# Starting a normed part of a transformer kernel: which engine splits the weights, into which buffers, and in what order

## The chip, the cores and the metric

The kernel runs on one core of a Trainium2 chip. The metric is the device time of one launch in microseconds (us); lower is better. It is written in Tile, which places the semaphores and the buffers; the order of the instructions is the compiler's, but for the stretches that the code marks as ordered by hand.

## What is computed

256 tokens of 1024 features go through eight parts, one after the other, all in float32: a SwiGLU feed-forward, a hybrid mixer, two feed-forwards, a sparse attention, a feed-forward, and two three-branch mixers. Each part normalises its input, multiplies it with a wide weight matrix, and adds its result to the residual `x`:

```python
def rms_norm(x, g):
    y = x * lax.rsqrt(jnp.mean(x * x, axis=-1, keepdims=True) + EPS) * g
for l in range(DEPTH):
    x = x + 0.5 * swiglu(rms_norm(x, ffn_norm[l, 0]), ...)
    h = rms_norm(x, mix_norm[l])
    x = x + (hybrid_mixer(h, ...) if l % 2 == 0 else sparse_attention(h, ...))
    x = x + 0.5 * swiglu(rms_norm(x, ffn_norm[l, 1]), ...)
```

The two three-branch mixers follow, with norms of the same form.

## The kernel before

**Products.** A float32 operand is held as the sum of two float32r parts, hi and lo, and a product is three matmuls (`mm3`, L273 to L278: hi hi, hi lo, lo hi). Weights come from memory in tiles `raw` of [128, 2048]; each is used as two halves of 1024 columns. `Net.halve` (L259) takes a pair of buffers, one of tag `hi` and one of tag `lo` (four of each), and `split` (L199) fills them: ScalarE (ACT) copies the 1024 columns into hi, and two subtractions of 512 columns make lo. The second of these goes to GpSimd (POOL) where `help` is set, and to VectorE (DVE) else.

**The start of a part.** `down_steps` (L333) is the last product of a part. It holds its last four weight halves a, b, c, d, and finishes one token tile at a time: `whole(t, a)`, `whole(t, b)` are six matmuls each, `last(t, cb)` is six more and then `done`, one DVE addition that writes 512 columns of `x` of token tile t. Between these products the next part is begun (class `Entry`, L47 to L101), in an order written out by hand (L370 to L407): `manual()` makes PE, DVE, ACT and POOL each keep the order in which the code names their work. A part either has its input normed first (`norm` is true: the hybrid, the sparse attention and the two last mixers, so four starts) or takes the norm later (the feed-forwards).

The steps of a normed start, for token tile t:

- `square(t, cb)` (L68): ACT squares 512 columns of `x` and sums them.
- `root(t)` (L79): two small POOL instructions (L212, L215) make 1/sqrt of the mean.
- `scale(t)` (L82): two DVE instructions (L85) of 512 columns multiply `x` by the root and the gain.
- `turn(t, b)` (L95): PE transposes four blocks of 128 columns (L433), ACT copies them out as the hi of the input (L201), DVE makes the lo (L205).
- `halve(i)` (L92): the split of half i of the part's first weights; i = 0, 1 come from the first `raw` tile, 2 and 3 from the second.
- `go(kk, t)` (L99): three matmuls with k-tile kk of token tile t and weight half kk // 2.

Before, in the four normed starts, `HELP[1]` is all ones, so that the second lo of each of the four halves is POOL's. The halves take their buffers from the tags `hi` and `lo`: these are held by a, b, c and d, so half 0 waits for the end of `whole(1, a)`, half 1 for that of `whole(1, b)`, and halves 2 and 3 for that of `last(1, 1)`.

**Other storage.** Wide work tiles come from tag `g` with 13 buffers of [128, 1024]. In a normed start after a feed-forward, the feed-forward's last hidden activations hold four of them and the start takes seven (gain 1, transposed input 4, scaled input 2).

Of the kernel before, what the change touches and what calls it, by code (L numbers as in the profile page):

```python
# [10 lines left out]
F32R = mybir.dt.float32r  # L11
# [4 lines left out]
PSUM = bass.MemoryType.PSUM  # L16

D = 1024
# [6 lines left out]
HELP = ((0, 0, 0, 0), (1, 1, 1, 1), (1, 1, 0, 0))  # L25
# [3 lines left out]
class Wide:  # L29
    """Transposed activations, split in two float32r parts: k-tiles of [128 features, 256 tokens]."""  # L30
# [16 lines left out]
class Entry:  # L47
    """The start of a part: its input, normed or not, transposed (times the gain), and its first
    512 columns. gain [128, 8], or all of it on every partition where the norm is taken here."""

    def __init__(self, net, i, norm, dram, between=None):
        self.net, self.nc, self.norm, self.first = net, net.nc, norm, not i
        self.raw, self.gain = [], net.gain
        self.load(dram[0], between)
        if not between:
            self.load(dram[1])
        if i:
            self.gain = net.g()
            self.nc.sync.dma_start(self.gain, net.ins["gains"][i])
        self.hT, self.w = Wide(net.g, 2), []  # L60
        self.ss = [net.small(2) for _ in range(2)]
        self.src, self.rstd = [net.g() for _ in range(2)] if i else net.x, [None, None]
        self.out = [net.ps() for _ in range(2)]
# [28 lines left out]
    def halve(self, i):  # L92
        self.w.append(self.net.halve(self.raw[i // 2], i % 2, HELP[2 if self.first else self.norm][i]))

# [8 lines left out]
class Net:  # L103
# [52 lines left out]
    def consts(self):  # L156
# [8 lines left out]
        self.tri = self.const(128)                   # [s, t] = s <= t  # L165
        nc.vector.tensor_scalar(self.tri, ij, 0.0, None, op0=OP.is_ge)
        self.after = self.const(128)                 # [s, t] = s > t
        nc.vector.tensor_scalar(self.after, ij, 0.0, None, op0=OP.is_lt)
        self.cap = self.const(128)                   # 0 where s <= t, else very negative
        nc.scalar.activation(self.cap, self.after, AF.Copy, scale=-BIG)  # L170
        # [t, s]: very large where s <= t, else very negative
# [13 lines left out]
    def narrow(self, dram, cols, hT, out):  # L185
        """A few columns of h @ W, token-major, into out[:, t, :]. dram: [128, 8 * cols]."""
# [20 lines left out]
    def rsqrt(self, v, n, scale=1.0, add=EPS):  # L207
        """1 / sqrt(v * scale + add), [128, n]; add may be a column."""
# [9 lines left out]
    def row_rstd(self, x):  # L218
        """[128, 1] of 1/sqrt(mean(x*x) + eps), x [128, 1024]."""
# [6 lines left out]
    def softplus(self, y, n):  # L226
        """max(y, 0) + log1p(exp(-|y|)); log1p(u) = 2 atanh(u / (2 + u)) as a series (|argument| <= 1/3)."""
# [31 lines left out]
    def halve(self, raw, h, help=False):  # L259
        """Half h of the columns as (hi, lo)."""  # L260
        self.n += 1
        c = raw.shape[-1] // 2
        hi = self.wp.tile([128, 1024], F32R, name=f"hi{self.n}", tag="hi", bufs=4)[:, :c]
        lo = self.wp.tile([128, 1024], F32R, name=f"lo{self.n}", tag="lo", bufs=4)[:, :c]
        self.split(hi, lo, raw[:, h * c:(h + 1) * c], help)
        return hi, lo

    def unit(self, dram, cols=2048, help=(0, 0)):
        """Load [128, cols], give two (hi, lo) halves."""
# [3 lines left out]
    def mm3(self, out, a, b, start, stop):  # L273
        """out += a^T b with a = (hi, lo), b = (hi, lo)."""
# [5 lines left out]
    def group_x(self, dram, hT):  # L280
        """512 columns of h @ W, token-major: one PSUM bank per token tile.
        dram: [2, 128, 2048] (k half; 4 k-tiles x 512 columns)."""
# [7 lines left out]
    def group_steps(self, dram, hT):  # L290
        """group_x in two steps, a yield in between."""
# [14 lines left out]
    def weave(self, main, side, done):  # L306
        """Emit main, with as many steps of side as it gives in between; done gets an item when main is through."""
# [7 lines left out]
    def group_w(self, dram, hT):  # L315
        """256 columns of h @ W, feature-major: two PSUM tiles, [128, :256] used.
        dram: [128, 2048] (8 k-tiles x 256 columns)."""
# [15 lines left out]
    def down_steps(self, dram, n, aT, done, then, ready={}, mid=lambda: None):  # L333
        """x-wide product: aT(kk, t) -> (hi, lo) stationary; dram [n/2, 128, 2048]
        (2 k-tiles x 1024 columns). done(t, cb, psum) when half a token tile is complete;
        the next part (then) starts as the last k-tiles, a token tile at a time, go through.
        mid finishes the second token tile of these."""
# [32 lines left out]
        with self.manual():  # L370
# [3 lines left out]
            if E.norm:  # L374
# [4 lines left out]
                E.root(0)  # L379
                E.scale(0)  # L380
                whole(1, a)
                E.halve(0)
                whole(1, b)
                last(1, 0)
                E.turn(0, 0)
                E.halve(1)
                last(1, 1)
                E.halve(2)
                E.turn(0, 1)
                E.square(1, 0)  # L390
                E.square(1, 1)
# [32 lines left out]
    def to_T(self, t, src, aT, gain=None):  # L424
        """src [128 tokens, 1024] -> k-tiles of aT for token tile t (times gain[:, k])."""
# [3 lines left out]
    def flip(self, src, aT, b, t, gain=None):  # L429
        """src [128 tokens, 512] -> half b of aT, token tile t."""  # L430
# [5 lines left out]
    def put_T(self, p, aT, b, t, gain):  # L436
        """Transposed [128, 4, 128] in PSUM (times gain) -> half b of aT, token tile t."""
# [4 lines left out]
        # the two engines take turns at a PSUM bank: each all of it at a time  # L442
# [37 lines left out]
    def start(self, dram):  # L480
        """The first part's start: loads in the order of their use; the clock of TensorE is up by then."""
# [57 lines left out]
class Hybrid:  # L539
    def hybrid(self, then):  # L540
# [8 lines left out]
        def products():  # L549
            """The wide products that only wait for the input: z, q, k, v and the output gate."""  # L550
# [30 lines left out]
        def chain():  # L581
            """Gives how many steps of the wide products may go in here."""
# [38 lines left out]
            bc = self.g().rearrange("p (j t c) -> p j t c", j=4, t=2)     # B0 B1 C0 C1  # L621
# [10 lines left out]
            def inputs(g):  # L632
                """x of one group of 8 heads, token-major, before its activation"""
# [9 lines left out]
            def states(g):  # L643
# [4 lines left out]
                # state after the first chunk: B^T (x dt decay)  # L648
# [7 lines left out]
            def decays(g):  # L656
                """per chunk of 128 tokens: scores times decays [s, head, t]"""
# [44 lines left out]
            # scores C B^T (transposed), B of the first chunk token-major  # L702
# [32 lines left out]
            R = self.t2()                   # R0 R1 wi wk rows  # L735
# [13 lines left out]
            w = self.small(16)              # exp(-m_t) (2 chunks), w_inter, state weights  # L749
# [25 lines left out]
            # state of the first chunk  # L775
# [55 lines left out]
def _parts(x, n, bits):  # L831
    """x as a sum of n float32 parts of so many significant bits."""
# [18 lines left out]
class Sparse:  # L851
    def rope_setup(self):
        """cos and sin of position * frequency, [128, 2, 32] each."""
# [14 lines left out]
        self.cs = self.const(128)           # cos (2 x 32), sin (2 x 32)  # L868
# [4 lines left out]
        # tables (c, s) times the gain of q; times that of k, and plain for the index key  # L873
# [15 lines left out]
    def rope(self, out, x, c, s, H, copies=1, help=0):  # L889
        """out[:, h, copy, :] = x rotated; c, s [128, H or 1, 2, 32] broadcast; x [128, H, 64]."""  # L890
# [14 lines left out]
    def sparse(self, then):  # L905
# [10 lines left out]
        kv = self.l2().rearrange("p (t c) -> p t c", t=2)  # L916
        wi = self.small(16).rearrange("p (t h) -> p t h", t=2)
        kT = self.l2().rearrange("p (i t s) -> p i t s", i=2, t=2)      # key, index key; twice over the partitions
        v = kv[:, :, 64:128]
        kk = self.t2().rearrange("p (h r d) -> p h r d", h=4, r=2)    # (t, i), twice  # L920
# [45 lines left out]
        def index_logits(t):  # L966
            S = 128 * (t + 1)
            for jb in range(2):
                for r in range(2):              # heads on one half of the partitions share a bank
# [23 lines left out]
        def choose(t, part):  # L993
            """The 64 largest scores of a row: 0 there, very negative elsewhere."""
# [49 lines left out]
        cat = Wide(self.f, 2)  # L1044

        def attend(t, g, b):
            """Some heads: scores with the bias, and their maxima."""
            S = 128 * (t + 1)
            per = 4 // (t + 1)                  # heads in one PSUM bank
            if b == 0:  # L1050
                state[t, g] = (v8(self.pt()), self.small(8), self.small(8), self.small(8))
            po, sm, mx, nm = state[t, g]        # by parity
# [22 lines left out]
        def probs(t, g, b):  # L1075
            """Their transposes."""
# [8 lines left out]
        def values(t, g, b):  # L1085
            """Their products with the values."""
# [51 lines left out]
class Second:  # L1138
    def second_setup(self):
        nc, V, A, G = self.nc, self.nc.vector, self.nc.scalar, self.nc.gpsimd  # L1140
        self.rtri = self.const(128)                  # [s, t] = s >= t
        V.tensor_tensor(self.rtri, self.after, self.ident, OP.add)
        self.before = self.const(128)                # [s, t] = s < t
        V.tensor_tensor(self.before, self.tri, self.ident, OP.subtract)
        self.rcap = self.const(128)                  # 0 where s >= t, else very negative
# [9 lines left out]
        self.near = self.load_const("near", 128)     # in one block of 32  # L1155
        self.eye = self.load_const("eye", 512)       # [q, i] = 2 q + (p / 32) % 2 == i
        rel = self.t2(512, I32)
        G.iota(rel.rearrange("p (j i) -> p j i", j=2), pattern=[[-128, 2], [1, 256]], base=0, channel_multiplier=-1)
        self.rel = self.const(512)                   # [j, i] = i - j
        G.tensor_copy(self.rel, rel)  # L1160
        # log sigmoid of the decays: [128, layer, direction, head]
# [6 lines left out]
    def second(self, l, then, end=None):  # L1168
# [13 lines left out]
        # ================= gated delta rule =================  # L1182
        def delta(y_c):
            """Gives how many steps of the other branches may go in here."""
# [15 lines left out]
            V.reciprocal(beta, eb)                   # [t, direction, head]  # L1200
            gs = self.small(16)                      # log decays: [direction, t, head]
# [583 lines left out]
```

## Time and profile before

| | |
|---|---|
| median of 3 runs | 1735.54 us |
| lowest and highest of them | 1732.81 and 1738.21 us |
| span of the profiled execution | 1757.1 us |
| instructions in it | 23334 |

The page gives no other time for the profiled execution than its span, which is 21.6 us above the median of the runs. In the views below, PE is TensorE, PEld its weight loads, DVE VectorE, ACT ScalarE, POOL GpSimd. A time "from the span's start" is where an instruction stood in this execution. PEclk is the granted clock of TensorE as a share of 2.4 GHz.

### The profile page before, as it was taken

To read this page: it belongs to the slowest core of one execution; us is meant where nothing else is said; L and a number is where in the kernel's file an instruction comes from. 1 tells how busy PE (TensorE), PEld (TensorE's weight loads), DVE (VectorE), ACT (ScalarE), POOL (GpSimd) and SP (SyncE) were. 2 spreads that over 40 slices of the span, in tenths; PEclk is the share of its full clock that TensorE was granted. 3 is DMA by queue.
4 is the path that set the end of the run, shared out by engine and by line. 5 is a ranking of instruction groups with operands and counts; after the bars stand their busy time and mean duration, and the time that the engine had idled before them with its cause. 6 is when DMAs were issued, how large, how long until landed. Compare 5 with 4: busy or idle time off the path is not lost.

```text
span 1757.1 us, 23334 instructions
## 1 busy us (share of the span) xinstructions
PE 1720.3 (98%) x8742; PEld 1437.8 (82%) x8742; DVE 1111.6 (63%) x2107; ACT 902.7 (51%) x1323; POOL 318.1 (18%) x466
## 2 busy tenths in 40 slices
PE   9999999999999999999899999999999999999998
PEld 7888799887888888887688888788898878879886
DVE  6555588666555565547736564557775765678565
ACT  6544476465444454435445544466446446745643
POOL 3000121001000100002311000233632124264211
PEclk9999999999999999999669999999999999999999
DMA  7545453445455554554114555455544444544442
GB/s 269 189 173 199 146 192 121 144 158 185 173 191 191 180 184 176 193 188 151 40 66 174 192 174 216 140 174 168 156 145 150 158 155 168 168 134 167 156 144 96
DMA packets 63425, 287.40 MB, mean 164 GB/s; under 512 B 23760, under 2 KB 26704, under 8 KB 30288
## 3 DMA queue, kind: packets, MB, share of 16 engines
q1 hardware_dynamic: 63312, 285.92, 46.5%
q8 instruction: 68, 1.11, 0.3%
q14 instruction: 45, 0.37, 0.1%
HBM read 283.28 MB, written 2.62 MB: 163 GB/s over the span
## 4 chain that ended last, share of the span: by engine, by line
PE 81%; POOL 6%; DVE 4%; issue 4%; DMA 2%; ACT 2%; SPq 1%; POOLq 0%; ACTq 0%; DVEq 0%
PE mm L277 24%; PE mm L278 24%; PE mm L276 24%; POOL g L1320 2%; POOL g L1318 2%; PE tr L433 1%; PE tr L468 1%; DMA g<-dram 1%; ACT hi L201 1%; DVE lo L205 1%; POOL lo L205 1%; DMA dram<-g 1%; DVE g L85 1%; POOL sm L215 0%; DVE g L987 0%
## 5 line engine op out<-in xcount | busy, mean ns | idle before, releaser
L205 DVE TENSOR_TENSOR lo<-raw,hi 128x512 fp32r<-128x512 f32 (+1 forms) x1024 | 694.8, 720 | 406.1 <-ACT hi L201 404.6
L201 ACT ACTIVATE hi<-raw 128x1024 fp32r<-128x1024 f32 x530 | 551.5, 1045 | 455.3 <-PE mm L278 317.7
L277 PE MATMUL mm<-lo,g 128*128 128x512 f32 (+1 forms) x1440 | 576.9, 401 | 0.8 <-DVE lo L205 0.5
L276 PE MATMUL mm<-hi,g 128*128 128x512 f32 (+1 forms) x1440 | 576.5, 403 | 0.7 <-ACT g L201 0.7
L278 PE MATMUL mm<-hi,g 128*128 128x512 f32 (+1 forms) x1440 | 571.5, 397 | 0.3 <-DVE g L446 0.2
L278 PEld LDWEIGHTS mm<-hi,g 128*128 128x128 f32 x1440 | 273.8, 190 | 62.8 <-DVE g L205 1.6
L277 PEld LDWEIGHTS mm<-lo,g 128*128 128x128 f32 x1440 | 274.0, 190 | 61.5 <-DVE lo L205 3.9
L276 PEld LDWEIGHTS mm<-hi,g 128*128 128x128 f32 x1440 | 273.9, 190 | 60.2 <-ACT g L201 1.2
L277 PE MATMUL mm<-lo,f 128*128 128x512 f32 x416 | 165.2, 397 | 0.2 <-POOL lo L205 0.2
L278 PE MATMUL mm<-hi,f 128*128 128x512 f32 x416 | 164.8, 397 | 0.0
L276 PE MATMUL mm<-hi,f 128*128 128x512 f32 x416 | 163.6, 400 | 0.0
L276 PE MATMUL mm<-g,hi 128*128 128x256 f32 x480 | 136.3, 284 | 0.0
L278 PE MATMUL mm<-g,lo 128*128 128x256 f32 x480 | 135.8, 285 | 0.0
L277 PE MATMUL mm<-g,hi 128*128 128x256 f32 x480 | 135.2, 282 | 0.0
L212 POOL TENSOR_SCALAR sm<-sm 128x1 f32<-128x1 f32 x18 | 9.4, 521 | 562.2 <-ACT c L70 561.1
L277 PEld LDWEIGHTS mm<-lo,f 128*128 128x128 f32 x416 | 78.4, 188 | 19.0 <-POOL lo L205 0.6
L278 PEld LDWEIGHTS mm<-hi,f 128*128 128x128 f32 x416 | 78.3, 188 | 18.5
L276 PEld LDWEIGHTS mm<-hi,f 128*128 128x128 f32 x416 | 78.5, 189 | 18.2
L276 PEld LDWEIGHTS mm<-g,hi 128*128 128x128 f32 x480 | 90.6, 189 | 0.7 <-issue 0.2
L277 PEld LDWEIGHTS mm<-g,hi 128*128 128x128 f32 x480 | 90.5, 189 | 0.3
L278 PEld LDWEIGHTS mm<-g,lo 128*128 128x128 f32 x480 | 90.1, 188 | 0.4 <-issue 0.2
L201 ACT ACTIVATE g<-tr 128x512 fp32r<-128x512 f32 x48 | 28.1, 595 | 86.9 <-PE tr L433 57.1
(387 smaller groups left out, 1693.9 us busy)
## 6 DMA issues: line engine op xcount, KB each, us to landing
raw<-in_wgu_dram SPq DMA_DIRECT2D x86, 1024.0 KB, 4.8
raw<-in_wdn_dram SPq DMA_DIRECT2D x44, 1024.0 KB, 4.8
raw<-in_bx_dram SPq DMA_DIRECT2D x24, 1024.0 KB, 4.9
raw<-in_bgate_dram SPq DMA_DIRECT2D x24, 1024.0 KB, 4.9
raw<-in_bw_dram SPq DMA_DIRECT2D x20, 1024.0 KB, 5.0
raw<-in_hyx_dram SPq DMA_DIRECT2D x12, 1024.0 KB, 4.8
raw<-in_bproj_dram SPq DMA_DIRECT2D x12, 1024.0 KB, 5.0
raw<-in_hyw_dram SPq DMA_DIRECT2D x10, 1024.0 KB, 4.8
```

The lines of the kernel that those rows point to most:

```text
L85: self.nc.vector.scalar_tensor_tensor(self.src[t][:, s], self.net.x[t][:, s], self.rstd[t], self.gain[:, s], op0=OP.mult, op1=OP.mult)
L201: nc.scalar.activation(hi, src, AF.Copy)
L205: (nc.gpsimd if o and help else nc.vector).tensor_tensor(lo[..., s], src[..., s], hi[..., s].bitcast(F32), OP.subtract)
L212: G.tensor_scalar(r, v, add, EPS, op0=OP.add, op1=OP.add)
L276: mm(out, a[0], b[0], start=start, stop=False)
L277: mm(out, a[0], b[1], start=False, stop=False)
L278: mm(out, a[1], b[0], start=False, stop=stop)
L433: self.nc.tensor.transpose(p[:, k, :], src[:, k * 128:(k + 1) * 128], self.ident)
L468: nc.tensor.transpose(p[:, t, j, :], hd[:, j * 128:(j + 1) * 128], self.ident)
L1318: G.tensor_tensor(a, Z[:, :m, e:e + 1].to_broadcast([128, m, n]), B[:, e:e + 1, cs].to_broadcast([128, m, n]), OP.mult)
L1320: G.tensor_tensor(Z[:, :m, cs], Z[:, :m, cs], a, OP.add)
```

## The change

The flag for a normed part no longer selects a row of `HELP`: only the very first part, which is not one of the four, has POOL's help. `Net.halve` can be given a pair of buffers, and half 1 gets two of tag `g`. The hand-written order of a normed start is another. Comments and docstrings are gone too.

```diff
-HELP = ((0, 0, 0, 0), (1, 1, 1, 1), (1, 1, 0, 0))
+HELP = ((0, 0, 0, 0), (1, 1, 0, 0))
...
-    def halve(self, i):
-        self.w.append(self.net.halve(self.raw[i // 2], i % 2, HELP[2 if self.first else self.norm][i]))
+    def halve(self, i, spare=False):
+
+        self.w[i] = self.net.halve(self.raw[i // 2], i % 2, HELP[self.first][i],
+                                   [self.net.g(1024, F32R) for _ in range(2)] if spare else None)
...
-    def halve(self, raw, h, help=False):
+    def halve(self, raw, h, help=False, home=None):
...
-        hi = self.wp.tile([128, 1024], F32R, name=f"hi{self.n}", tag="hi", bufs=4)[:, :c]
-        lo = self.wp.tile([128, 1024], F32R, name=f"lo{self.n}", tag="lo", bufs=4)[:, :c]
+        hi, lo = home or (self.wp.tile([128, 1024], F32R, name=f"{p}{self.n}", tag=p, bufs=4)[:, :c] for p in ("hi", "lo"))
...
                 last(0, 1)
                 E.square(0, 1)
                 E.root(0)
+                E.halve(1, True)
+                whole(1, a)
                 E.scale(0)
-                whole(1, a)
                 E.halve(0)
                 whole(1, b)
+                E.turn(0, 0)
                 last(1, 0)
-                E.turn(0, 0)
-                E.halve(1)
+                E.square(1, 0)
+                E.halve(2)
                 last(1, 1)
-                E.halve(2)
+                E.square(1, 1)
                 E.turn(0, 1)
-                E.square(1, 0)
-                E.square(1, 1)
                 E.root(1)
                 E.halve(3)
                 E.scale(1)
```

After these lines, unchanged: `go(0, 0)` to `go(6, 0)`, `turn(1, 0)`, `go(7, 0)`, `turn(1, 1)`, and the eight `go(kk, 1)`.

## Rows read from the trace of the kernel before

**Rows 1.** The page, parts 1 and 4: busy time by engine; the chain that ended last.

```profile
PE 1720.3 (98%) x8742; PEld 1437.8 (82%) x8742; DVE 1111.6 (63%) x2107; ACT 902.7 (51%) x1323; POOL 318.1 (18%) x466
...
PE 81%; POOL 6%; DVE 4%; issue 4%; DMA 2%; ACT 2%; SPq 1%; POOLq 0%; ACTq 0%; DVEq 0%
```

**Rows 2.** Waits of PE, whole span: total us, times, longest us.

```profile
PE tr L433 <- DVE g L85: 8.1, 8, 1.8
```

**Rows 3.** Windows, the four normed starts: us, PE busy (instructions), PEclk, DMA share, GB/s.

```profile
194.64:210.09 15.45, 13.38 (x66) 1.00 0.26 82
789.89:805.33 15.44, 13.36 (x65) 1.00 0.16 40
1116.96:1133.44 16.48, 14.44 (x65) 0.93 0.30 103
1429.95:1445.28 15.33, 13.37 (x66) 1.00 0.27 86
```

**Rows 4.** Timeline of PE, first normed start: start us, duration us, instruction, idle before it.

```profile
197.42 0.40 PE L276 MATMUL mm<-hi,g 128*128 128x512 f32 x1
...
198.58 0.40 PE L278 MATMUL mm<-hi,g 128*128 128x512 f32 x1
199.28 0.66 PE L433 MATMUL tr<-c,g 128*128 128x128 f32 x4 [0.30 <-DVE g L85]
199.69 0.48 PE L276 MATMUL mm<-hi,g 128*128 128x512 f32 x1
...
201.52 0.48 PE L276 MATMUL mm<-hi,g 128*128 128x512 f32 x1
...
206.38 0.40 PE L278 MATMUL mm<-hi,g 128*128 128x512 f32 x1
208.54 0.66 PE L433 MATMUL tr<-c,g 128*128 128x128 f32 x4 [1.76 <-DVE g L85]
208.95 0.48 PE L276 MATMUL mm<-hi,g 128*128 128x512 f32 x1
...
209.73 0.60 PE L433 MATMUL tr<-c,g 128*128 128x128 f32 x4
210.09 0.48 PE L276 MATMUL mm<-hi,g 128*128 128x512 f32 x1
```

**Rows 5.** Timeline of DVE, just before and in the first normed start.

```profile
187.63 1.29 DVE L205 TENSOR_TENSOR lo<-raw,hi 128x512 fp32r<-128x512 f32 x2 [1.49 <-ACT hi L201]
...
197.46 2.43 DVE L85 SCALAR_TENSOR_TENSOR g<-x,sm,g 128x512 f32<-128x512 f32 x2 [1.92 <-POOL sm L215]
...
202.81 1.19 DVE L205 TENSOR_TENSOR lo<-raw,hi 128x512 fp32r<-128x512 f32 x1
```

**Rows 6.** Timeline of POOL, first normed start.

```profile
196.85 0.57 POOL L215 TENSOR_TENSOR sm<-sm,c 128x1 f32<-128x1 f32 x1
197.39 1.29 POOL L205 TENSOR_TENSOR lo<-raw,hi 128x512 fp32r<-128x512 f32 x1
201.59 3.57 POOL L205 TENSOR_TENSOR lo<-raw,hi 128x512 fp32r<-128x512 f32 x2 [2.92 <-ACT hi L201]
```

**Rows 7.** The line of the scalings, whole span: duration ns, shortest, median, longest.

```profile
L85 DVE SCALAR_TENSOR_TENSOR g<-x,sm,g x16: 736/1240/1797, 197.5 to 1443.5; 128x512 f32<-128x512 f32 x16
```

**Rows 8.** Timeline of ACT, first normed start.

```profile
196.25 1.04 ACT L201 ACTIVATE hi<-raw 128x1024 fp32r<-128x1024 f32 x1
199.97 0.60 ACT L201 ACTIVATE g<-tr 128x512 fp32r<-128x512 f32 x1 [2.68 <-PE tr L433]
200.47 2.00 ACT L201 ACTIVATE hi<-raw 128x1024 fp32r<-128x1024 f32 x2
...
202.84 0.63 ACT L70 ACTIVATE c<-x 128x512 bf16<-128x512 f32 x1
...
203.59 0.63 ACT L70 ACTIVATE c<-x 128x512 bf16<-128x512 f32 x1
```

**Rows 9.** Window, third normed start after its long wait: engines' busy us, PEclk, DMA.

```profile
1131.21:1134.62 3.41, 3.41 (x13) 2.83 (x12) 1.32 (x3) 2.90 (x4) 0.00 (x0) 0.50 0.91 312
```

More of the change, by code (lines that the diff above doesn't have):

```diff
@@ L59, in __init__ @@
             self.nc.sync.dma_start(self.gain, net.ins["gains"][i])
-        self.hT, self.w = Wide(net.g, 2), []
+        self.hT, self.w = Wide(net.g, 2), {}
         self.ss = [net.small(2) for _ in range(2)]
```

## The prediction

> **What bounds the kernel now.** I read the page first. PE is busy for 1720.3 of 1757.1 us and carries 81% of the chain that ended last [rows 1], so the change can only matter through the time that PE stands still or runs slowly. The list of PE's waits then says where: the largest entry, 8.1 us in eight waits, is transposes waiting for the scalings of L85 [rows 2], two in each of the four normed starts that the change touches. So I went to those four stretches, each from PE's end of token tile 0 (`whole(1, a)` begins) to the first `go` of token tile 1. They last 15.45, 15.44, 16.48 and 15.33 us [rows 3], and the third is longer because the clock fell in it (0.93 granted on average).
>
> The first start serves as the pattern. PE stands still three times in it [rows 4]. Matmuls follow each other by 0.232 us (five steps from 197.42 to 198.58), so PE could go on at 198.81, but the transposes of `turn(0, 0)` start at 199.28: 0.47 us. Between 201.52 and 206.38 lie 20 matmul steps, which take 4.73 with the 0.09 that the first after transposes takes longer (208.95 to 209.73 is 0.78 for three): 0.13 us lost, waiting for a lo. After 206.38 PE is free at 206.61, and `turn(1, 0)` starts at 208.54: 1.93 us. Sum 2.53 us, four times: some 10 us is all that a better order could give back, plus one clock fall.
>
> **Where those waits come from.** DVE's row [rows 5] shows the scalings of tile 0 starting at 197.46, when POOL's root ends (196.85 + 0.57) [rows 6]. The first lets its transposes go at 199.28, so it took about 1.78 us, against a shortest of 0.74 for the same instruction [rows 7]; POOL's split at 197.39 ran beside it. The lo at 202.81 took 1.19, beside POOL's pair of 3.57 us, against 0.60 a step for the pair of lo's at 187.63, ahead of POOL's work. So POOL's splits slow DVE, and taking them off frees about 1.1 us of DVE in each pair of scalings and 0.5 in that lo.
>
> The Trainium skill has a rule that speaks against the change: "Perfetto Trace Analysis", section "Optimizing Scalar/DVE Operations", says that work may well be given to GpSimd where DVE is saturated, with the warning that the two share a read port, so that it may not help. By the advice alone the four moved splits, 2.4 us of DVE in a start (0.60 each), would be lost, 9.6 us in all; by the warning they cost less than the 2.7 us that the rows give back.
>
> In sum DVE's time in a start hardly changes; what decides is which wait each split is put in front of.
>
> **The change, queue by queue, in the clock of the first start.** All four engines keep the written order, so each time is the later of "queue free" and "input there", plus 0.04 us for a signal. Steps: DVE 0.60 (0.69 to the result, 0.74 for a scaling); ACT 0.96 for a hi of 1024 columns (1.04 to the result: the pair at 200.47 takes 2.00), 0.50 for a hi out of transposes (0.60 to the result), 0.75 for a square [rows 5, 7, 8]. An engine's other costs are those of before.
>
> *Half 1 in its own buffers.* It needs no release, so ACT makes its hi at 196.25, where half 0 stood, ready at 197.29. DVE now does both its lo's before the scalings: 197.33 and 197.93. The cover for this is gone: before, DVE was idle there until 197.46, waiting for the root. The scalings therefore start at 198.53 instead of 197.46, though now at 0.74 us each: the first is there at 199.27, as good as before (199.24). *`turn(0, 0)`* thus starts at 199.31 on PE, but it has moved ahead of `last(1, 0)`: PE asks for it at 197.42, six matmuls earlier, and stands still for **1.89 us** instead of 0.47.
>
> *Splits of half 0.* DVE goes on without a pause: scaling 2 at 199.13, lo's of half 0 at 199.73 and 200.33, lo of `turn(0, 0)` at 200.93, and only then the addition of `last(1, 0)`, at 201.53, though PE had it ready at about 201.4. Result 202.22.
>
> *Squares of tile 1, and halves 2 and 3.* ACT's square starts at 202.25, and behind it stands the hi of half 2, 203.0 to 204.04 (its buffers, those of b, are long free). DVE's two lo's follow at 204.08 and 204.68. **The addition of `last(1, 1)` stands behind them**, at 205.28, though PE had it ready at 202.8. Result 205.97; second square at 206.0; and behind this, on ACT, the hi of `turn(0, 1)`: 206.75 to 207.35, its lo on DVE 207.39 to 208.07. Then the hi of half 3, 207.25 to 208.29, lo's at 208.33 and 208.93, scalings of tile 1 at 209.53, the first there at 210.27. The root, two POOL instructions of 0.9 us in sum, is done by 207.9 and hidden by half 3.
>
> *PE.* `turn(0, 0)` 199.31 to 199.72; twelve matmuls to 202.59; `turn(0, 1)` to 202.95; `go(0)` to `go(3)` need only `turn(0, 0)`, to 205.82. `go(4)` needs the hi of `turn(0, 1)`, at 207.39: **1.57 us**, and its third matmul the lo: 0.26. `go(4)` to `go(6)` end at 209.73; `turn(1, 0)` waits for the scaling until 210.31: 0.58. With `go(7)` and both transposes (1.55 us, as 208.54 to 210.09) the first `go` of tile 1 is at 211.86, against 210.09. Stalls 4.30 instead of 2.53: **1.8 us more per start.**
>
> *Costed at nothing.* The other two additions and the non-normed starts are unchanged. The first weight tile is released about 2 us earlier, the second about 2 us later, as PE itself is; these two fetches are SP's next work, and the DMA share is 0.16 to 0.30 in these stretches [rows 3], so neither is late. The two `g` tiles make 4 + 7 + 2 = 13 of 13 buffers: just enough; if one were missing, half 1 would hold up ACT until `last(1, 1)` has gone through. A buffer pair of the `hi` and `lo` tags stays free for the next weights; PE has no wait there now, so it gains nothing. The compiler orders the rest of each part afresh; I allow 3 us either way for it.
>
> **The clock.** In the third start the clock fell after the wait at `turn(1, 0)`: 1131.21 to 1134.62 at 0.50, that is 1.2 GHz [rows 9], and the start is 1.03 us longer than the first [rows 3] up to a point inside that window; half of the 3.41 us, 1.7, is the upper bound. I take 1.5 us a fall. Four such long stalls gave one fall; eight (1.89 and 1.57 + 0.26 per start) give two by the same rate.
>
> **The sum.** Four starts at 1.8 are 7.2 us; one fall of before is not there by itself (minus 1.5), two new ones come (3.0): plus 8.7 in a span of 1757.1. The runs are 1.2% shorter than that span; scaled, plus 8.6 on 1735.5: **1744 us**. With no fall it is 1741, and 0.4 us of error per start (two or three signals and steps) moves it by 1.6.
>
> **The rivals.**
> 1. *Late half covered, no change.* If the addition of `last(1, 1)` reached its square before the splits of half 2, the stall at `go(4)` would vanish, and with it the one at `turn(1, 0)`: per start +1.42 at `turn(0, 0)`, +0.1 at a lo, minus 2.06, or minus 0.54; four of these and the fall of before replaced by one: about 1733. What decides is whether DVE keeps the written order; in the kernel before it does so in all four starts. Chance 0.17.
> 2. *Faster: DVE's relief wins.* If the idle 1.92 us before the scalings [rows 5] took in half 1's two lo's and the scalings still began at 197.46, at 0.74, `turn(0, 0)` could go at 198.2 (0.8 us of stall), everything behind it on DVE came 1.1 us earlier, and the later stalls shrank to some 0.5: 1.3 against 2.53, minus 1.2 times four and the fall: 1729. It turns on the hi of half 1 being ready by 196.2. Against it: ACT cannot begin that before the second square ends at 196.3. Chance 0.10.
> 3. *Slower still: the clock falls often.* If six of the eight stalls bring a fall: 7.2 + 9.0 - 1.5 = 14.7, 1750; if all do, 1753. "TensorE: Matmul & The Clock Gate", Part 1, in the Trainium skill, says that the throttled state is the default and activity lifts it, so each new stall may bring a fall; the trace agrees for one long stall in four. Chance 0.18.
> 4. *A `g` buffer is missing,* or the compiler's new order elsewhere costs more than 3 us: above 1755, chance 0.05.
>
> **The numbers.** Forecast 0.50, 1739 to 1748. A measurement can tell about 0.3%, 5.2 us, from no change. Slower takes nearly all of the forecast, rival 3 and rival 4: 0.68. Same takes rival 1 and a low tail of the forecast: 0.20. Faster is rival 2 and the luck of rival 1: 0.12. The range from 1733 to 1753 takes in the forecast, rival 1's time and rival 3.
>
> **What would show it.** Right: in each start DVE has two lo's before the scalings, PE waits about 1.9 us at the first transposes and about 1.6 at the fifth k-tile (on ACT's hi), and hardly 0.6 at `turn(1, 0)`; the first `go` of tile 1 comes about 17.2 us after `whole(1, a)`; POOL has sixteen instructions of L205 fewer. Wrong: the additions stand ahead of the splits in DVE's row, or the four stretches are shorter than before, or the time goes somewhere outside them.

## The result, and the profile after

The changed kernel takes 1745.99 us, median of 14 runs, against 1737.08 us of 14 runs of the kernel before: a ratio of 1.007 [1.0052, 1.0088], 8.9 us slower. The prediction was 1744 (plus 8.6).

The profile of before on which the prediction rested was an unlucky one: from 861.6 to 906.0 us, in the sparse attention, TensorE's clock was granted at 0.50, 1.2 of its 2.4 GHz, and a second profiled execution of the same kernel has 1.00 there and a span of 1735.2 us. Runs of these kernels lie in groups some 20 us apart; that this stretch makes the groups is likely, but was not shown. So the changed kernel's profile (span 1743.5, its own run 1745.5) is compared with that second one (span 1735.2, its own run 1737.94).

In code and profile of the changed kernel the lines stand one or two lower: L207 makes a lo, L203 a hi, L434 transposes, L277 to L279 multiply, L477 is the addition of `last`, L214 and L217 are the root. The first rows are the page's part 1 and the chain that ended last, against [rows 1]:

```profile
PE 1700.1 (98%) x8742; PEld 1417.3 (81%) x8742; DVE 1115.4 (64%) x2123; ACT 904.7 (52%) x1325; POOL 293.5 (17%) x450
...
PE 83%; POOL 5%; DVE 5%; ACT 3%; issue 3%; DMA 1%; SPq 0%; POOLq 0%; ACTq 0%; DVEq 0%
```

PE is still the bound. POOL has 16 instructions fewer and DVE 16 more: the second lo of each of the four halves of a start has changed engine. The windows of the four starts follow, first of the second profile of before (us, PE busy, PEclk, DMA share, GB/s):

```profile
195.43:210.89 15.46, 13.38 (x66) 1.00 0.27 84
...
1409.99:1425.32 15.33, 13.36 (x66) 1.00 0.26 84
sum 61.66, PE 53.49; mean PE 13.37
```

and of the changed kernel:

```profile
194.86:212.10 17.24, 13.76 (x65) 1.00 0.23 75
792.29:809.53 17.24, 13.78 (x65) 1.00 0.14 38
1101.33:1118.56 17.23, 13.73 (x65) 1.00 0.24 76
1413.68:1430.98 17.30, 13.72 (x65) 1.00 0.25 78
sum 69.01, PE 55.00; mean PE 13.75
```

They explain most of the result: 69.01 less 61.66 is 7.35 us, of 8.3 by which the two spans differ. The clock is full in all eight; the fall in the third start of [rows 3] was not there a second time. The list of PE's waits of the changed kernel says where the 1.8 us per start are lost (total us, times, longest):

```profile
PE tr L434 <- DVE g L85: 8.5, 8, 1.9
PE mm L277 <- ACT g L203: 6.3, 6, 1.4
PE tr L1040 <- POOL t L904: 5.3, 1, 5.3
```

The first line is of the size of [rows 2], but it is another wait: the long one now stands at the first transposes. The second is new. (The third, in the sparse attention, stands in the second profile of before too, with 5.2 us; the last experiment uses it.) PE's row in the first start, with the idle time and its releaser in brackets, to be read beside [rows 4]:

```profile
197.41 0.40 PE L279 MATMUL mm<-hi,g 128*128 128x512 f32 x1
199.56 0.66 PE L434 MATMUL tr<-c,g 128*128 128x128 f32 x4 [1.75 <-DVE g L85]
...
205.81 0.40 PE L279 MATMUL mm<-g,g 128*128 128x512 f32 x1
207.62 0.50 PE L277 MATMUL mm<-hi,g 128*128 128x512 f32 x1 [1.42 <-ACT g L203]
...
209.86 0.40 PE L279 MATMUL mm<-hi,g 128*128 128x512 f32 x1
210.56 0.65 PE L434 MATMUL tr<-c,g 128*128 128x128 f32 x4 [0.31 <-DVE g L85]
...
212.10 0.48 PE L277 MATMUL mm<-hi,g 128*128 128x512 f32 x1
```

DVE's row says what the two long waits wait for:

```profile
197.55 1.29 DVE L207 TENSOR_TENSOR g<-raw,g 128x512 fp32r<-128x512 f32 x2 [1.80 <-ACT g L203]
198.76 1.41 DVE L85 SCALAR_TENSOR_TENSOR g<-x,sm,g 128x512 f32<-128x512 f32 x2
...
204.37 1.29 DVE L207 TENSOR_TENSOR lo<-raw,hi 128x512 fp32r<-128x512 f32 x2 [1.80 <-ACT hi L203]
205.58 0.69 DVE L477 SCALAR_TENSOR_TENSOR x<-mm,x 128x512 f32<-128x512 f32 x1
207.60 0.69 DVE L207 TENSOR_TENSOR g<-tr,g 128x512 fp32r<-128x512 f32 x1 [1.33 <-ACT g L203]
```

At 197.55 stand half 1's two lo's, and the scalings come behind them. At 204.37 stand half 2's, and behind them, at 205.58, the addition of `last(1, 1)`, whose last matmul PE had begun at 202.60. Its square, and ACT's hi of `turn(0, 1)` behind the square, are late with it, and that hi is what PE's `go(4)` waits for. Before, the addition stood ahead of half 2's lo (first profile of before, whose start begins 0.22 us earlier):

```profile
202.21 0.68 DVE L476 SCALAR_TENSOR_TENSOR x<-mm,x 128x512 f32<-128x512 f32 x1
```

The pair of scalings itself takes 1.41 us where it took 2.43 [rows 5].

### The profile page after: what moved, and what is told of

It reads as the page before. It is cut to its first block, busy times and chain, and to the rows that moved or that the text cites. A ratio compares the mean times of both kernels' runs of the same rounds, so it can differ in the third digit from the quotient of the medians.

```text
span 1743.5 us, 23290 instructions
## 1 busy us (share of the span) xinstructions
PE 1700.1 (98%) x8742; PEld 1417.3 (81%) x8742; DVE 1115.4 (64%) x2123; ACT 904.7 (52%) x1325; POOL 293.5 (17%) x450
## 4 chain that ended last, share of the span: by engine, by line
PE 83%; POOL 5%; DVE 5%; ACT 3%; issue 3%; DMA 1%; SPq 0%; POOLq 0%; ACTq 0%; DVEq 0%
PE mm L278 24%; PE mm L279 24%; PE mm L277 24%; POOL g L1319 2%; POOL g L1321 2%; DVE lo L207 1%; PE tr L434 1%; PE tr L469 1%; ACT hi L203 1%; DMA g<-dram 1%; ACT c L70 0%; DVE g L85 0%; DVE g L988 0%; PE tr L1253 0%; PE tr L1378 0%
## 5 line engine op out<-in xcount | busy, mean ns | idle before, releaser
L207 DVE TENSOR_TENSOR lo<-raw,hi 128x512 fp32r<-128x512 f32 (+1 forms) x1032 | 700.4, 721 | 405.0 <-ACT hi L203 403.2
L203 ACT ACTIVATE hi<-raw 128x1024 fp32r<-128x1024 f32 (+1 forms) x526 | 547.2, 1045 | 451.1 <-PE mm L279 311.0
L277 PE MATMUL mm<-hi,g 128*128 128x512 f32 (+1 forms) x1424 | 569.5, 402 | 6.3 <-ACT g L203 6.3
L278 PE MATMUL mm<-lo,g 128*128 128x512 f32 (+1 forms) x1424 | 567.9, 399 | 0.7 <-DVE lo L207 0.5
L279 PE MATMUL mm<-hi,g 128*128 128x512 f32 (+1 forms) x1424 | 564.6, 397 | 0.2 <-DVE g L447 0.2
L277 PEld LDWEIGHTS mm<-hi,g 128*128 128x128 f32 x1424 | 270.1, 190 | 65.9 <-ACT g L203 8.5
L279 PEld LDWEIGHTS mm<-hi,g 128*128 128x128 f32 x1424 | 269.6, 190 | 63.9 <-DVE g L207 2.6
L278 PEld LDWEIGHTS mm<-lo,g 128*128 128x128 f32 x1424 | 270.0, 190 | 60.0 <-DVE lo L207 2.5
L279 PE MATMUL mm<-hi,f 128*128 128x512 f32 x416 | 164.2, 395 | 0.0
L277 PE MATMUL mm<-hi,f 128*128 128x512 f32 x416 | 163.3, 400 | 0.0
L277 PE MATMUL mm<-g,hi 128*128 128x256 f32 x480 | 136.4, 285 | 0.9 <-ACT hi L203 0.9
L279 PE MATMUL mm<-g,lo 128*128 128x256 f32 x480 | 135.5, 283 | 0.0
L214 POOL TENSOR_SCALAR sm<-sm 128x1 f32<-128x1 f32 x18 | 7.8, 436 | 599.9 <-ACT c L70 599.1
L279 PEld LDWEIGHTS mm<-hi,f 128*128 128x128 f32 x416 | 78.1, 188 | 18.7
L277 PEld LDWEIGHTS mm<-hi,f 128*128 128x128 f32 x416 | 78.1, 188 | 18.3
L277 PEld LDWEIGHTS mm<-g,hi 128*128 128x128 f32 x480 | 90.3, 188 | 1.9 <-ACT hi L203 1.2
L279 PEld LDWEIGHTS mm<-g,lo 128*128 128x128 f32 x480 | 90.3, 188 | 0.3 <-issue 0.2
L203 ACT ACTIVATE g<-tr 128x512 fp32r<-128x512 f32 x48 | 28.1, 595 | 77.8 <-PE tr L434 48.0
```

The costliest lines, as they stand in the source:

```text
L203: nc.scalar.activation(hi, src, AF.Copy)
L207: (nc.gpsimd if o and help else nc.vector).tensor_tensor(lo[..., s], src[..., s], hi[..., s].bitcast(F32), OP.subtract)
L214: G.tensor_scalar(r, v, add, EPS, op0=OP.add, op1=OP.add)
L277: mm(out, a[0], b[0], start=start, stop=False)
L278: mm(out, a[0], b[1], start=False, stop=False)
L279: mm(out, a[1], b[0], start=False, stop=stop)
```

## The experiments

Two theories had to be told apart. Mine: the time is lost by the order, by what stands in front of what on DVE and ACT. The rival: it is lost because DVE does work that POOL did. Where only the order of the hand-written stretch differs, the diff shows that order against the changed kernel's.

**The old order, POOL off.** The changed kernel with the order of before; half 1 keeps its buffers of tag `g`.

```diff
 E.root(0)
-E.halve(1, True)
+E.scale(0)
 whole(1, a)
-E.scale(0)
 E.halve(0)
 whole(1, b)
-E.turn(0, 0)
 last(1, 0)
-E.square(1, 0)
-E.halve(2)
+E.turn(0, 0)
+E.halve(1, True)
 last(1, 1)
-E.square(1, 1)
+E.halve(2)
 E.turn(0, 1)
+E.square(1, 0)
+E.square(1, 1)
```

> The change with the hand-written order of before put back: all splits on DVE, half 1 in buffers of its own. Order theory (what costs time is which work stands behind which on DVE and ACT, above all the addition of last(1, 1) behind the two lo's of half 2): with POOL no longer in DVE's way, the first scaling is ready before PE asks, and the stretch from whole(1, a) to the first go of tile 1 is 13.9 us in each start (15.4 before, 17.2 after); four times minus 1.5 us and perhaps one clock fall less: 1729 to 1732 beside 1737 for the kernel before. Load theory (four more subtractions on a full DVE are what costs): at least as slow as the changed kernel, stretches of 17 us, 1744 to 1746. Buffer theory (the two g tiles and the free pair rearrange what follows, and that costs): stretches shorter, but the runs within 3 us of the changed kernel's 1746.

**The same with half 1 in the usual buffers** (`E.halve(1)`), so that only the end of POOL's help is left of the change.

> Like e1_old_order, with half 1 in a pair of the hi and lo tags as in the kernel before; so the only thing that is left of the change is that the splits are off POOL. Order theory: half 1 is not asked for before its pair is free, so the stretch is 13.9 us as in e1_old_order, 1729 to 1732. Load theory: 17 us, 1744 to 1746. Buffer theory: faster than e1_old_order by 3 us or more.

The windows of the four starts of this second kernel:

```profile
195.02:208.81 13.79, 13.30 (x66) 1.00 0.30 95
...
1404.81:1418.65 13.84, 13.25 (x66) 1.00 0.30 97
sum 55.14, PE 53.17; mean PE 13.29
```

The first kernel's four starts sum to 55.13. So without POOL, in the old order, the starts are 6.5 us *shorter* than before (61.66), and the buffers of half 1 are worth nothing there. The rival theory is wrong in sign. DVE's row of the second kernel shows how:

```profile
197.84 1.41 DVE L85 SCALAR_TENSOR_TENSOR g<-x,sm,g 128x512 f32<-128x512 f32 x2 [1.92 <-POOL sm L217]
...
203.37 1.28 DVE L207 TENSOR_TENSOR lo<-raw,hi 128x512 fp32r<-128x512 f32 x2
...
205.25 1.29 DVE L207 TENSOR_TENSOR lo<-raw,hi 128x512 fp32r<-128x512 f32 x2
206.46 1.41 DVE L85 SCALAR_TENSOR_TENSOR g<-x,sm,g 128x512 f32<-128x512 f32 x2
```

From 203.37 on it works without a gap, and with four steps more than before still reaches the second scalings 11.44 us after the window's start (206.46 less 195.02), before 12.11 (207.54 less 195.43, by the second profile of before). The whole times show less of this gain than the traces: 1735.93 (1.0019 [0.9986, 1.0052]) and 1733.06 (0.9997 [0.9962, 1.0033]), both the same as before and above the 1729 to 1732 expected. Their profiled executions took 1729.25 and 1730.19; five of twelve runs of each took 1749.5 to 1754, with a mean granted clock of 0.977 to 0.981 against 0.988 to 0.996 of the others. The last experiment goes after those.

**The new order with POOL's help.** The changed kernel, with the second lo of each half back on POOL.

```diff
-HELP = ((0, 0, 0, 0), (1, 1, 0, 0))
+HELP = ((0, 0, 0, 0), (1, 1, 1, 1), (1, 1, 0, 0))
...
-        ... HELP[self.first][i],
+        ... HELP[2 if self.first else self.norm][i],
```

> The changed kernel with POOL's help as before: four second lo's per start are POOL's again. Order theory: the stalls stay and POOL gets in the way of the lo's and scalings besides: the stretch is 17.2 to 18.6 us, 1746 to 1751. Load theory: DVE is relieved of four subtractions (2.4 us) per start, the stretch falls to 15.4 us, 1737 to 1740. Buffer theory: like the changed kernel, within 2 us.

1750.14 us, 1.0078 [1.0063, 1.0093], as the order theory expected; the starts sum to 72.06, one of them with a clock fall. DVE's row in the first start:

```profile
198.41 3.44 DVE L85 SCALAR_TENSOR_TENSOR g<-x,sm,g 128x512 f32<-128x512 f32 x2
```

The same pair takes 3.44 us beside POOL's lo's and 1.41 without. So POOL's help costs under either order, 1.6 us a start in the old one (61.66 less 55.14, a quarter of it), some 0.7 in the new (17.90 against 17.24 in the first start).

**Half 2 behind the second square.** The changed kernel, one step moved.

```diff
 E.square(1, 0)
-E.halve(2)
 last(1, 1)
 E.square(1, 1)
+E.halve(2)
 E.turn(0, 1)
```

> The changed kernel with half 2 behind the second square of tile 1, so that the addition of last(1, 1) no longer stands behind the two lo's of half 2. Order theory: the hi of turn(0, 1) is ready about 1.2 to 1.4 us earlier, and since that chain set the stretch, it falls from 17.2 to 15.8 to 16.1 us; the stall at the first transposes stays at 1.9 us; 1740 to 1742. Load theory: the same work on the same engines, 17.2 us and 1746. If the stall at the first transposes set the stretch: 17.2 us too.

1741.85 us, 1.004 [1.0019, 1.0061]. Two of the entries in the list of PE's waits, and DVE's row in the first start:

```profile
PE tr L434 <- DVE g L85: 7.1, 4, 1.8
PE mm L279 <- DVE g L207: 2.8, 4, 0.7
```

```profile
202.96 0.69 DVE L477 SCALAR_TENSOR_TENSOR x<-mm,x 128x512 f32<-128x512 f32 x1 [0.46 <-PE mm L279]
205.45 1.29 DVE L207 TENSOR_TENSOR lo<-raw,hi 128x512 fp32r<-128x512 f32 x2 [1.80 <-ACT hi L203]
```

The addition now goes as soon as PE is ready, 202.96 instead of 205.58, and no start waits for ACT's hi at `go(4)` any more. The starts sum to 64.30, 4.7 less than after, and 16.0 to 16.2 each, near the 15.8 to 16.1 expected. What is left is the wait of 1.8 us at the first transposes, four times, and one of 0.7 for a lo. The late part of the loss, the larger one, is thus shown to come from half 2's place.

**Half 1 behind the scalings.** The changed kernel, with the split that it had put first put back.

```diff
 E.root(0)
-E.halve(1, True)
 whole(1, a)
 E.scale(0)
+E.halve(1, True)
 E.halve(0)
```

> The changed kernel with half 1 behind the scalings of tile 0 on DVE (nothing else moved). Order theory, in the form that the late chain (addition of last(1, 1), square, hi of turn(0, 1)) sets the stretch: the stall at the first transposes falls from 1.9 to about 0.8 us, but DVE does the same work in sum before that chain, so the stall at the fifth k-tile grows by as much, 1.6 to about 2.8 us: the stretch stays at 17.2 us, 1745 to 1746. If instead each stall adds by itself: 16.1 us and 1741.

1756.39 us (four runs, 1748.15 to 1768.98), 1.0117 [1.0084, 1.0151]: the slowest of all, and above the 1745 to 1746 expected. Two entries of the list of PE's waits, and DVE's row in the first start:

```profile
PE mm L277 <- ACT g L203: 11.0, 6, 2.6
PE tr L434 <- DVE g L85: 3.1, 5, 0.8
```

```profile
197.57 1.41 DVE L85 SCALAR_TENSOR_TENSOR g<-x,sm,g 128x512 f32<-128x512 f32 x2 [1.92 <-POOL sm L217]
...
205.60 0.68 DVE L477 SCALAR_TENSOR_TENSOR x<-mm,x 128x512 f32<-128x512 f32 x1
207.61 0.69 DVE L207 TENSOR_TENSOR g<-tr,g 128x512 fp32r<-128x512 f32 x1 [1.33 <-ACT g L203]
```

The scalings begin 1.2 us earlier (197.57 against 198.76) and the first transposes with them, but the late addition stands at 205.60 against 205.58: PE only waits longer at `go(4)`, 2.60 us instead of 1.42. The early stall is not a loss of its own while the late chain is as it is. What makes this kernel slower than the changed one is mostly the clock. Three of its four windows:

```profile
194.76:212.88 18.12, 14.85 (x65) 0.91 0.26 90
793.41:810.75 17.34, 13.76 (x66) 1.00 0.15 38
...
1425.31:1443.74 18.43, 15.12 (x65) 0.91 0.29 94
```

The one start without a fall lasts 17.34, as after; the three with one lose 0.8 to 1.1 us each (the third, not shown, lasts 18.19). In sum the starts are 3.1 us longer than the changed kernel's, of 10.8 by which the spans differ (1754.3 and 1743.5). Another 6.4 lie in the sparse attention, where the clock was granted at 0.50 from 866.9 to 880.3 us: the same instructions took 22.68 us (866.26 to 888.94) against 16.24 in the changed kernel (865.10 to 881.34). The profile of the new order with POOL's help has the same 22.68 us there, so the 1750 of that kernel isn't made in its starts alone either.

**An order worked out by the same arithmetic.** Half 1's hi between the two squares of tile 0, `turn(0, 0)` behind `last(1, 0)`, half 2 behind `last(1, 1)`, half 3 ahead of the last square.

```diff
 E.square(0, 0)
 last(0, 1)
+E.halve(1, True)
 E.square(0, 1)
 E.root(0)
-E.halve(1, True)
 whole(1, a)
 E.scale(0)
 E.halve(0)
 whole(1, b)
-E.turn(0, 0)
 last(1, 0)
-E.square(1, 0)
-E.halve(2)
+E.turn(0, 0)
 last(1, 1)
-E.square(1, 1)
+E.halve(2)
+E.square(1, 0)
 E.turn(0, 1)
-E.root(1)
 E.halve(3)
+E.square(1, 1)
+E.root(1)
 E.scale(1)
```

> A new order, all splits on DVE, half 1 in its own buffers: ACT makes half 1's hi between the two squares of tile 0, so that DVE does its lo's while it waits for the root; turn(0, 0) stands behind last(1, 0) again; the addition of last(1, 1) stands ahead of half 2. Order theory: PE stands still for less than 0.3 us in each start, the stretch is 12.9 to 13.2 us (15.4 before): four times minus 2.4 and one fall less, 1726 to 1728 where the clock holds in the attention. Load theory: DVE has the same 20 instructions as in the changed kernel, so 17 us.

A miss: 1735.15 us, 1.0008 [0.9984, 1.0032], and starts of 14.18, 14.46, 14.10 and 14.30 us, 57.04 in all, longer than the old order's 55.14. POOL's row in the first start points to the reason:

```profile
196.65 0.80 POOL L214 TENSOR_SCALAR sm<-sm 128x1 f32<-128x1 f32 x1 [150.54 <-ACT c L70]
197.53 0.57 POOL L217 TENSOR_TENSOR sm<-sm,c 128x1 f32<-128x1 f32 x1
204.49 1.40 POOL L214 TENSOR_SCALAR sm<-sm 128x1 f32<-128x1 f32 x1 [6.39 <-ACT c L70]
205.97 0.55 POOL L217 TENSOR_TENSOR sm<-sm,c 128x1 f32<-128x1 f32 x1
```

against the changed kernel's, where DVE stands idle at that moment:

```profile
196.67 0.32 POOL L214 TENSOR_SCALAR sm<-sm 128x1 f32<-128x1 f32 x1 [150.42 <-ACT c L70]
...
207.19 0.29 POOL L214 TENSOR_SCALAR sm<-sm 128x1 f32<-128x1 f32 x1 [9.54 <-ACT c L70]
```

An instruction on one column takes 0.80 and 1.40 us instead of 0.3: it ends at 197.45 and 205.89, just behind DVE's runs of lo's (195.97 to 197.26, 204.27 to 205.72). The order had put DVE's work exactly where the root falls, and the root is what the scalings wait for (spans on POOL are rough, but the DVE rows behind them show the wait: 0.87 and 0.83 us of idle time, released by L217). No run moved the root alone to test this.

**The sparse attention's clock held up.** Three kernels, each with matmuls that nobody reads, on PE, ahead of two sets of transposes in the attention (`flip`): 32 where PE waits 5.2 us for POOL's rope, and 4 at a later wait. One has only POOL's help taken off, one is the changed kernel, one the kernel before.

```diff
         def flip(g, t):
             pT = self.pt()
+            for _ in range({(0, 1): 32, (1, 0): 4}.get((g, t), 0)):
+                mm(pT[:, :256].rearrange("p (t c) -> p t c", t=2), hT.tok(0, 0)[0], hT.both(0)[0], start=True, stop=True)
```

> The kernel with only POOL's help taken off, with 32 matmuls of 256 columns that nobody reads ahead of the sparse attention's second query transposes (where PE waits 5.2 us for POOL's rope and the granted clock then is 0.50 for 10 us), and 4 ahead of the third ones. If the groups of runs some 20 us apart come from a clock that falls in this stretch after a wait of PE, the low clock at 845 and at 861 both vanish, no run lies at 1750, and all runs agree within some 6 us, at 1720 to 1727. Rival: the groups have another cause (a transfer, another stretch); then runs at 1745 to 1753 stay, about 5 of 12.

> The changed kernel with the same added matmuls. With the attention's clock held the difference to the kernel with only POOL's help taken off is that of the four starts alone: 3.5 to 4 us for each of the four by the in-order arithmetic (stretch 17.2 against 13.4 to 13.8), so 14 to 16 us slower: 1734 to 1742. Rival: most of the difference of the medians came from the attention; then under 8 us.

> The kernel before with the same added matmuls. With the attention's clock held it is 4 times 1.8 = 7 us faster than the changed kernel with them (6 to 10), and 6 to 8 us slower than the kernel with only POOL's help taken off with them. Rival: the difference between the two kernels was made outside the starts; then under 4 us.

Medians 1729.5 (0.995 [0.9917, 0.9983]), 1746.12 (1.0048 [1.0032, 1.0065]) and 1736.82 (0.999 [0.9978, 1.0002]). The times are above those expected, but the differences are near them: the changed kernel is 9.3 us behind the kernel before (6 to 10 expected) and 16.6 behind the one with only POOL's help off (14 to 16), which is 7.3 ahead of the kernel before (6 to 8). The starts give 69.02, 61.65 and 55.15, that is 7.4, 13.9 and 6.5 of these. Most of each difference is made in the starts.

The part on the clock came half true. The window behind the 5.2 us wait, of the kernel with only POOL's help off, first without the added matmuls, then with them:

```profile
841.00:850.00 9.00, 8.49 (x24) 0.50 0.22 67
```

```profile
841.00:850.00 9.00, 6.82 (x28) 0.81 0.22 63
```

The low clock behind the 5.2 us wait is shorter, but not gone (PE still stands idle for 2.18 us there, at 845.33, waiting for a lo), and the median is above the 1720 to 1727 that I had written. Of the twelve runs eleven lie between 1725.76 and 1735.93, one at 1746.27; without the added matmuls it was five of twelve at 1749.5 and above. That speaks for the clock of this stretch as the cause of the groups, but one run in twelve is still far out, so it isn't settled. The kernel with only POOL's help off and the added matmuls is the one kernel here that is faster than before beyond its interval.

## Why the prediction was right

*The order's cost: right, nearly to the step.* Moved by the 0.22 us by which the first start begins later (194.86 for 194.64), the predicted times and the measured ones are: first transposes 199.53 and 199.56; `go(4)` 207.61 and 207.62; `turn(1, 0)` 210.53 and 210.56; first `go` of tile 1 212.08 and 212.10. The stalls, predicted 1.89, 1.57, 0.26 and 0.58, were 1.92 (199.56 less 197.41 and a step of 0.23), 1.58, 0.16 and 0.47. Per start 1.8 was predicted, and 1.84 measured (7.35 over four). The four engines do keep the written order, so in-order arithmetic with the steps of the trace before was enough.

*POOL's relief: right that it does not pay for the order.* The prediction took 2.7 us of DVE per start as freed against 2.4 added, so that DVE's time hardly changes; DVE is busy for 11.16 us of the first start in the second profile of before and for 11.30 in the changed kernel. A pair of scalings gave back 1.02 us (2.43 less 1.41) where 1.1 was priced. The old order without POOL shows the freed time as a real gain of 1.6 us a start, and all of it and 1.8 more lost to the new order: 55.14 to 69.01, 3.5 a start. All sixteen scalings of the changed kernel take 742 to 748 ns where [rows 7] had up to 1797. "SBUF — State Buffer", "Who interferes with whom", in the Trainium skill, says that a DVE instruction with two SBUF inputs contends with a GpSimd instruction that reads SBUF; the 3.44 against 1.41 us of the pair agrees. The weighing of "Perfetto Trace Analysis", "Optimizing Scalar/DVE Operations", in the Trainium skill, came out for the warning: by the advice alone the splits taken off POOL would have cost 9.6 us, and they gave back 6.5.

*The clock: wrong.* One fall taken off and two put in was the term that made 7.2 into 8.7. None of the four starts after has a fall, and the one of before did not come again in its second profile, behind the same wait of 1.76 us. By the idle times of the profiles, the changed kernel's waits of 1.75 and 1.42 us brought none in eight, the four of 2.2 to 2.3 us in the new order with POOL's help one, and the four of 2.5 to 2.6 us in the kernel with half 1 late three. The rate of one in four came from one trace of four starts, too few to carry a term. The median moved by 8.9 although that term was nought; 7.35 of it is the starts, and the other 1.6 isn't placed: the spans of the two traces leave only 0.95 outside the starts, which is within what single runs differ by. That the forecast of 8.6 met the 8.9 so closely is therefore luck: 7.2 of it was worked out, and the 1.5 of the clock stood in for something that isn't placed.

*The scale: unneeded.* Of the 21.6 us by which the span lay above the median, 20.0 come from one stretch at half clock, 861.6 to 906.0 (43.40 us where the second profile takes 23.39 for the same instructions), which lies outside the code that the change touches. The prediction scaled by 1.2% where it should have subtracted; here that moved 0.1 us, since the sum was small.

*The rivals.* 1, the late half covered: DVE kept the written order, and the addition stood behind half 2's lo's in all four starts; the kernel with half 2 late shows what it would have been like, except that its starts are 0.66 us longer than before (64.30 less 61.66, a quarter of it) instead of 0.54 shorter, mainly because half 2's lo's then stood ahead of the lo of `turn(0, 1)`: the wait for that lo was 0.88 (207.40 less 206.29 and a step of 0.23), where the prediction priced 0.1 in place of the 0.13 of before. 2, DVE's relief wins: not in this order, whose scalings began only at 198.76; a gain of this size is what the old order without POOL gives, by another way. 3, frequent clock falls: not in this kernel; the kernel with half 1 late has three in four starts, behind longer waits, and they cost it 0.8 to 1.1 us each there. 4: nothing of the kind.

## What to carry to other kernels

Where engines keep the written order, write the queue of each engine out with the steps of the trace and look at what stands in front of the work that others wait for: here two lo's of 1.2 us ahead of an addition delayed PE by 1.6 us by way of ACT. A change that bundles a gain with a loss can be taken apart by putting back one part at a time; the order of before with POOL off was there for the taking, with starts 6.5 us shorter in sum, though its median showed that only with the attention's clock held up. And before a single trace is used as the base, look at its clock: a stretch at half speed that a second execution doesn't have must not be priced as the kernel's.

## What was not expected of the hardware

- One stretch of the attention ran at half clock for 44 us, with PE busy throughout, and at full clock in another execution of the same kernel. In the profile of before and in its second one:

```profile
861.60:906.00 44.40, 44.40 (x169) 0.50 0.04 10
```

```profile
861.60:892.00 30.40, 29.62 (x194) 1.00 0.07 22
```

The second window holds more work: the instructions from the transposes at 861.03 to the product at 904.43 (43.40 us) are in the other execution those from 863.38 to 886.77 (23.39 us). In the first PE had stood still 1.16 us before these transposes, in the second 0.78. The other profiles without the added matmuls fall on the same two sides: in the two with a wait of 1.15 and 1.16 us at this place (the new order with POOL's help, and half 1 late) the clock fell behind it, to 0.50 for 13.4 us; in the five with 0.48 to 1.02 us it stayed full. No run changed this wait alone, so it isn't shown to be the cause.
- A POOL instruction on one column ended only behind DVE's run of lo's, 1.40 us instead of 0.29 (in the old order without POOL 0.44, from 204.37 on, behind a pair of lo's that ended at 204.65): taking POOL's large work away doesn't free its small work from DVE.
- Waits of 1.42 and 1.75 us in a row of dense matmuls left the clock full eight times of eight in the changed kernel, while one of 1.76 us was followed by a fall in the first profile of before; 2.5 to 2.6 us was followed by half clock in three of four starts, for about 3.4 us each (the window 207.70:211.10 of the first start was granted 0.51).
